# A convolution kernel's first image load, issued as 32 rows on one DMA queue and 96 rows on another

## The chip, the cores and the metric

The kernel runs on one core of one Trainium2 chip. The metric is the device time of one execution in microseconds (us); less is better. A core has five engines that run their own programs and meet at semaphores: TensorE (PE, matrix products into PSUM), VectorE (DVE), ScalarE (ACT), GpSimd (POOL) and SyncE (SP). Transfers between the main memory and the on-chip memory (SBUF, 128 partitions) are issued as DMAs by an engine's program and carried out by 16 DMA engines. In the profile "SPq" is SP's own sequencer, where DMAs are issued and semaphores waited for, and likewise for the other engines.

## The reference

A 3 x 3 convolution with padding 1 over 16 images of 64 channels and 64 x 64 pixels, to 64 output channels, with a residual added. All in float32:

```python
x_pad = np.pad(x, ((0, 0), (0, 0), (pad, pad), (pad, pad)), mode='constant')
for b, co, ci, kh, kw in ...:
    output[b, co] += weight[co, ci, kh, kw] * x_pad[b, ci, kh:kh+h, kw:kw+w]
return (output + residual).astype(np.float32)
```

The images, the residual and the result have 16.78 MB each.

## The kernel before

**Tiling.** Two images make a pair, which is 128 rows (2 x 64 channels) of 4096 pixels, one row for each SBUF partition, 16 KB a row and 2.1 MB a pair. There are eight pairs. The image pairs are loaded into three buffers `xr[0..2]` in turn (`NXR = 3`); the residual lies in one tile `ro` that holds all eight pairs and receives the result in place, so it is also what is stored. ACT casts each image to bfloat16 in two halves (even and odd pixel rows, L174 and L178) into one of four buffers `xp`. PE multiplies: for each image six weight tiles, each against four chunks of eight packed rows (L221 to L238). DVE adds the result in PSUM to the residual (L203), in two halves for each image.

**The weights.** `wraw` holds the raw weights (128 rows of 1152 bytes). PE transposes them in nine steps with an identity matrix that POOL builds (L216), and ACT and DVE copy the results as bfloat16 into `wl` (L183 and L190). The first product of the convolution needs `wl` and the first two casts.

**SP's program.** SP issues every DMA. For each pair p it issues the image load (`load_x`, L72), and after pairs 0, 1, 3, 5 and 7 a residual load (`load_ro`, L77), which brings one or two pairs. Right behind the load of pair 0 stands the weight load (L138). From pair 3 on SP first waits until the casts of pair p-3 have read its buffer (L135). After the loads it issues the stores (L80): three of two pairs each, each behind a wait for DVE's adds, and two of one pair at the end.

**The front.** Programs begin with a short preamble, in which each engine comes to a barrier with a drain; the kernel's own instructions follow it. The function `to_the_front` takes the DMA issued last, removes it from where it stands and inserts it into the first block of the program, ahead of that engine's own drain (L112 to L119):

```python
front = nc.main_func.blocks[0].instructions
at = next(
    i for i, e in enumerate(front) if e.engine == ins.engine and isinstance(e, mybir.InstDrain)
)
```

Before, only the load of pair 0 is moved so, in SP's program (L137).

**The semaphores of the image loads.** Each buffer `xr[i]` has a semaphore `s_x[i]`, to which each finished load adds 16. ACT waits for it ahead of the even image of a pair (L173), for 16 times the number of loads that the buffer has seen.

Of the kernel before, what the change touches and what calls it, by code (L numbers as in the profile page):

```python
# [15 lines left out]
def kernel(  # L16
# [7 lines left out]
    nc = tc.nc  # L24
# [11 lines left out]
    NXR = 3  # L36
# [7 lines left out]
    x_bc = x.rearrange("b c h w -> (b c) (h w)")  # L44
# [7 lines left out]
    xr = [nc.alloc_sbuf_tensor(f"xr{i}", [128, NPIX], FP32) for i in range(NXR)]  # L52
# [8 lines left out]
    s_x = [sem(f"s_x{i}") for i in range(NXR)]  # L61
# [6 lines left out]
    s_conv = sem("s_conv")  # L68
    s_add = sem("s_add")

    def load_x(p):
        return nc.sync.dma_start(out=xr[p % NXR][:, :], in_=x_bc[128 * p : 128 * p + 128, :]).then_inc(s_x[p % NXR], 16)  # L72

    def load_ro(i):
        if i >= 2:
            nc.sync.wait_ge(s_r[i % 2], 16 * (i // 2))
        nc.sync.dma_start(out=ro[:, RES[i], :], in_=res_bc[:, RES[i], :]).then_inc(s_r[i % 2], 16)  # L77

    def store(pairs):
        return nc.sync.dma_start(out=out_bc[:, pairs, :], in_=ro[:, pairs, :])  # L80

    def matmul(out_, lhsT, rhs, start, stop, ldweights):

        e = nc.tensor
        if ldweights:
            return e.matmul(out=out_, lhsT=lhsT, rhs=rhs, start=start, stop=stop, skip_group_check=True)  # L86
        return e.add_instruction(  # L87
            mybir.InstMatmult(
                name=nc.get_next_instruction_name(),
                engine=PE,  # L90
                ins=[e.lower_ap(rhs), e.lower_ap(lhsT)],
                outs=[e.lower_ap(out_)],
                start_tensor_calc=start,
                stop_tensor_calc=stop,
                tile_size=(128, 128),
                tile_position=(0, 0),
                bass_skip_group_check=True,
                ldweights=False,
            )
        )  # L100

    def to_the_front(dma):

        def fixed(ap):
            t = ap.bass_ap.tensor.name
            return mybir.PhysicalAccessPattern(
                ap=ap.ap, offset=ap.bass_ap.offset, dtype=ap.dtype, memref=t, memsetref=t + "_set", bass_ap=ap.bass_ap
            )  # L110

        front = nc.main_func.blocks[0].instructions  # L112
        here = nc.cur_bb.bb.instructions
        ins = here.pop()
        assert ins.name == dma.ins.name
        at = next(
            i for i, e in enumerate(front) if e.engine == ins.engine and isinstance(e, mybir.InstDrain)
        )
        front.insert(at, copy.replace(ins, ins=[fixed(a) for a in ins.ins], outs=[fixed(a) for a in ins.outs]))  # L119
# [5 lines left out]
    def weight_block(h, half, d, par, kh):  # L125

        at = 64 * half + 32 * h
        return dict(out=wl[at : at + 32, d, :, par, :], in_=tp[0:32, kh, 0:384].rearrange("p (kw co h) -> p kw co h", kw=3, h=2)[:, :, :, h])

    with tc.tile_critical(no_gpsimd_drain=True):  # L130

        for p in range(NPAIR):
            if p >= NXR:

                nc.sync.wait_ge(s_half, 2 * (p - NXR) + 3)  # L135
            if p == 0:
                to_the_front(load_x(p))  # L137
                nc.sync.dma_start(out=wraw[:, :], in_=w_rows[:, :]).then_inc(s_w, 16)  # L138
            else:
                load_x(p)  # L140
            if p in (0, 1, 3, 5, 7):
                load_ro((p + 1) // 2)
        for k in range(NEARLY):
            nc.sync.wait_ge(s_add, 4 * k + 5)
            store(slice(2 * k, 2 * k + 2)).then_inc(s_out, 16)


        nc.gpsimd.memset(ident[:, :], 0.0).then_inc(s_id, 1)  # L148
        nc.gpsimd.wait_ge(s_id, 1)
        nc.gpsimd.affine_select(  # L150
            out=ident[:, :],
            in_=ident[:, :],
            compare_op=mybir.AluOpType.not_equal,
            fill=1.0,
            base=0,
            pattern=[[-1, 128]],
            channel_multiplier=1,
        ).then_inc(s_id, 1)
        nc.gpsimd.wait_ge(s_id, 2)
        for t in xp:  # L160
            nc.gpsimd.memset(t[0:64, 0, :], 0.0).then_inc(s_id, 1)  # L161
            nc.gpsimd.memset(t[64:128, J, :], 0.0).then_inc(s_id, 1)  # L162
        nc.gpsimd.memset(wl[0:64, 0, :, 1, :], 0.0).then_inc(s_id, 1)  # L163
        nc.gpsimd.memset(wl[64:128, 1, :, 0, :], 0.0).then_inc(s_id, 1)  # L164


        for n in range(B):
            p, im = divmod(n, 2)
            hp = slice(64 * im, 64 * im + 64)
            x4 = xr[p % NXR].rearrange("q (j two w) -> q j two w", two=2, w=W)  # L170
            t = xp[n % NXP]
            if im == 0:
                nc.scalar.wait_ge(s_x[p % NXR], 16 * (p // NXR + 1))  # L173
            i = nc.scalar.copy(out=t[64:128, 0:J, :], in_=x4[hp, :, 0, :])  # L174
            i.then_inc(s_half, 1)
            if n >= NXP:
                i._wait_ge(s_conv, n - NXP + 1)
            nc.scalar.copy(out=t[0:64, 1 : J + 1, :], in_=x4[hp, :, 1, :]).then_inc(s_pack, 1)  # L178
            if n == 0:
                nc.scalar.wait_ge(s_id, NZERO + 1)  # L180
                for b in blocks[4:]:
                    for h in range(2):
                        i = nc.scalar.copy(**weight_block(h, *b))  # L183
                i.then_inc(s_id, 1)


        nc.vector.wait_ge(s_id, NZERO + 1)
        for k, b in enumerate(blocks[:4]):
            for h in range(2):
                i = nc.vector.tensor_copy(**weight_block(h, *b))  # L190
                if k == h == 0:
                    i.then_inc(s_bank, 2)
        i.then_inc(s_id, 1)
        for n in range(B):
            p, im = divmod(n, 2)
            hp = slice(64 * im, 64 * im + 64)
            o4 = ro[:, p, :].rearrange("q (j two w) -> q j two w", two=2, w=W)
            psj = ps[n % 2].rearrange("q c j w -> q (c j) w")
            if im == 0:
                i = next(i for i, pairs in enumerate(RES) if p < pairs.stop)  # L200
                nc.vector.wait_ge(s_r[i % 2], 16 * (i // 2 + 1))
            for par in range(2):
                i = nc.vector.tensor_tensor(  # L203
                    out=o4[hp, :, par, :], in0=psj[64 * par : 64 * par + 64, :, :], in1=o4[hp, :, par, :], op=ADD
                )
                if par == 0:
                    i._wait_ge(s_conv, n + 1)

                i.then_inc(s_add if par == 0 or n == B - 1 else s_bank, 1)


        nc.tensor.wait_ge(s_id, NZERO)
        nc.tensor.wait_ge(s_w, 16)
        wraw3 = wraw.rearrange("p (ci t) -> p ci t", t=9)
        for t in range(9):
            i = nc.tensor.transpose(  # L216
                out=tp[0:32, t // 3, 128 * (t % 3) : 128 * (t % 3) + 128], in_=wraw3[:, :, t], identity=ident[:, :]
            )
        i.then_inc(s_id, 1)
        nc.tensor.wait_ge(s_id, NZERO + 3)  # L220
        with nc.Fori(0, B // NXP, 1, engines=[PE]):  # L221
            for n in range(NXP):
                nc.tensor.wait_ge(s_bank, 1).then_inc(s_bank, -1)
                nc.tensor.wait_ge(s_pack, 1).then_inc(s_pack, -1)  # L224
                order = [(1, 0), (1, 1), (0, 0), (0, 1), (2, 0), (2, 1)]
                for i, (kw, d) in enumerate(order):
                    xlo, xhi = max(0, 1 - kw), min(W, W + 1 - kw)
                    for c in range(NCHUNK):
                        j0 = JC * c
                        m = matmul(  # L230
                            ps[n % 2][:, c, :, xlo:xhi],
                            wl[:, d, kw, :, :].rearrange("q r c -> q (r c)"),
                            xp[n][:, j0 + d : j0 + d + JC, xlo + kw - 1 : xhi + kw - 1],
                            i == 0,
                            i == len(order) - 1,
                            c == 0,
                        )
                m.then_inc(s_conv, 1)  # L238
# [37 lines left out]
```

## Time and profile before

| | |
|---|---|
| median of 3 runs | 122.76 us (122.69 to 122.91) |
| the profiled execution | 122.68 us |
| its span, first to last instruction | 120.8 us |
| PE busy (matmuls) | 87.9 us, 73% |
| DVE busy | 76.0 us, 63% |
| ACT busy | 63.1 us, 52% |
| POOL busy | 2.4 us, 2% |
| bytes moved by DMA | 50.48 MB: 33.70 read, 16.78 written |
| DMA packets | 3504, of which 304 are under 512 bytes |
| DMAs issued | 19, all by SP, on one queue |

The span is what the trace covers; about 1.9 us of the time lie outside it. The page divides the span into 40 slices of 3.02 us and gives for each the share in which each engine was busy, in tenths, and what the DMA engines moved. A query can give the same for windows of any length; there a DMA packet is counted where it begins, so a short window can show more than the engines can carry. For a DMA the trace has the time that its issue took on the engine's sequencer, and the time from the issue to the landing of its last byte. The first casts of the images run on ACT from 7.79 us, the transposes of the weights on PE from 8.27, and the first product of the convolution from 13.78; the last add ends at about 104.3 us.

### The profile page before, as it was taken

The numbers are of one execution on the slowest core, as the hardware profiler recorded it, in microseconds if no ns is written. First come the engines' busy times: TensorE is split into PE (matmuls) and PEld (weight loads), VectorE is DVE, ScalarE is ACT, GpSimd is POOL, SyncE is SP. The second block draws the span as 40 slices with busy tenths as digits, with TensorE's granted clock in tenths as the row PEclk, the third lists the DMA queues.
The fourth block names the chain that finished last, engine by engine and source line by source line (L and its number), as shares of the span: only waits on it lengthen the run. The fifth ranks groups of instructions, "written<-read, shape, count | busy, mean of one in ns | idle before, by whom it ended". The sixth has DMA issues, their size and how long they took to land.

```text
span 120.8 us, 734 instructions
## 1 busy us (share of the span) xinstructions
PE 87.9 (73%) x393; PEld 10.7 (9%) x105; DVE 76.0 (63%) x40; ACT 63.1 (52%) x37; POOL 2.4 (2%) x16
## 2 busy tenths in 40 slices
PE   0024499999999999999999999999999990000000
PEld 0011001101010011011111111011111100000000
DVE  0005400789898988989879898988989879500000
ACT  4049959948999923999960999883000000000000
POOL 5200000000000000000000000000000000000000
PEclk9999999999999999999999999999999999855555
DMA  7999999999999999999999999999999999999994
GB/s 168 428 428 428 428 428 434 428 434 434 428 434 434 434 428 434 434 434 434 434 434 423 423 428 434 423 412 434 434 434 434 423 434 434 434 428 434 434 434 174
DMA packets 3504, 50.48 MB, mean 418 GB/s; under 512 B 304, under 2 KB 432, under 8 KB 432
## 3 DMA queue, kind: packets, MB, share of 16 engines
q1 hardware_dynamic: 3504, 50.48, 98.5%
HBM read 33.70 MB, written 16.78 MB: 418 GB/s over the span
## 4 chain that ended last, share of the span: by engine, by line
PE 71%; DVEq 2%; DVE 2%; issue 0%
PE ps L87 53%; PE ps L86 18%; DVEq L130 2%; DVE ro L203 2%
## 5 line engine op out<-in xcount | busy, mean ns | idle before, releaser
L203 DVE TENSOR_TENSOR ro<-ps,ro 64x2048 f32<-64x2048 f32 x32 | 73.2, 2289 | 17.7 <-PE ps L87 17.2
L87 PE MATMUL ps<-xp,wl 128*128 128x504 bf16 (+1 forms) x288 | 80.0, 388 | 0.0
L86 PE MATMUL ps<-xp,wl 128*128 128x504 bf16 (+1 forms) x96 | 37.4, 389 | 3.4 <-PEq L224 3.4
L174 ACT CAST xp<-xr 64x2048 bf16<-64x2048 f32 x16 | 30.3, 1896 | 18.3 <-DMA xr<-in_x_dram 17.2
L178 ACT CAST xp<-xr 64x2048 bf16<-64x2048 f32 x16 | 30.4, 1897 | 0.4
L86 PEld LDWEIGHTS ps<-xp,wl 128*128 128x128 bf16 x96 | 9.5, 99 | 79.1 <-issue 79.1
L190 DVE CAST wl<-ps 32x192 bf16<-32x192 f32 x8 | 2.8, 348 | 10.6 <-PE ps L216 10.5
L216 PE MATMUL ps<-ident,wraw 128*32 128x128 f32 x9 | 2.1, 413 | 8.3 <-DMA wraw<-in_weight_dram 8.3
L216 PEld LDWEIGHTS ps<-ident,wraw 128*32 128x32 f32 x9 | 1.2, 137 | 8.7 <-issue 8.2
L174 ACT ACT_TABLE_LOAD x1 | 1.3, 1283 | 1.0 <-SPq L130 1.0
L183 ACT CAST wl<-ps 32x192 bf16<-32x192 f32 x4 | 1.2, 306 | 0.0
L162 POOL MEMSET xp<- 64x64 bf16 x4 | 0.6, 147 | 0.2
L161 POOL MEMSET xp<- 64x64 bf16 x4 | 0.6, 145 | 0.2
L150 POOL TENSOR_SCALAR_AFFINE_SELECT ident<-ident 128x128 f32<-128x128 f32 x1 | 0.3, 294 | 0.2 <-POOL ident L148 0.2
L164 POOL MEMSET wl<- 64x192 bf16 x1 | 0.3, 253 | 0.1
L163 POOL MEMSET wl<- 64x192 bf16 x1 | 0.3, 252 | 0.1
L148 POOL MEMSET ident<- 128x128 f32 x1 | 0.2, 205 | 0.6 <-SPq L130 0.6
L260 POOL MEMSET const-bfloat16-1.0<- 128x1 bf16 x1 | 0.1, 112 | 0.0
L260 POOL MEMSET const-uint8-127<- 128x1 uint8 x1 | 0.1, 112 | 0.0
L260 POOL MEMSET const-float32-0.0<- 128x1 f32 x1 | 0.1, 105 | 0.2 <-issue 0.2
L260 POOL MEMSET const-float32-1.0<- 128x1 f32 x1 | 0.1, 109 | 0.0
## 6 DMA issues: line engine op xcount, KB each, us to landing
xr<-in_x_dram SPq DMA_DIRECT2D x8, 2048.0 KB, 15.3
ro<-in_residual_dram SPq DMA_DIRECT2D x3, 4096.0 KB, 24.0
out_dram<-ro SPq DMA_DIRECT2D x3, 4096.0 KB, 33.2
ro<-in_residual_dram SPq DMA_DIRECT2D x2, 2048.0 KB, 15.9
out_dram<-ro SPq DMA_DIRECT2D x2, 2048.0 KB, 12.8
wraw<-in_weight_dram SPq DMA_DIRECT2D x1, 144.0 KB, 7.1
```

The lines of the kernel that those rows point to most:

```text
L86: return e.matmul(out=out_, lhsT=lhsT, rhs=rhs, start=start, stop=stop, skip_group_check=True)
L87: return e.add_instruction(mybir.InstMatmult(name=nc.get_next_instruction_name(), engine=PE, ins=[e.lower_ap(rhs), e.lower_ap(lhsT)], outs ...
L130: with tc.tile_critical(no_gpsimd_drain=True):
L161: nc.gpsimd.memset(t[0:64, 0, :], 0.0).then_inc(s_id, 1)
L162: nc.gpsimd.memset(t[64:128, J, :], 0.0).then_inc(s_id, 1)
L174: i = nc.scalar.copy(out=t[64:128, 0:J, :], in_=x4[hp, :, 0, :])
L178: nc.scalar.copy(out=t[0:64, 1 : J + 1, :], in_=x4[hp, :, 1, :]).then_inc(s_pack, 1)
L183: i = nc.scalar.copy(**weight_block(h, *b))
L190: i = nc.vector.tensor_copy(**weight_block(h, *b))
L203: i = nc.vector.tensor_tensor(out=o4[hp, :, par, :], in0=psj[64 * par : 64 * par + 64, :, :], in1=o4[hp, :, par, :], op=ADD)
L216: i = nc.tensor.transpose(out=tp[0:32, t // 3, 128 * (t % 3) : 128 * (t % 3) + 128], in_=wraw3[:, :, t], identity=ident[:, :])
L260: nc = _bacc.Bacc("TRN2", target_bir_lowering=False, num_devices=1)
```

## The change

The load of pair 0 becomes two DMAs. Rows 0 to 31 (0.52 MB) are issued by SP, in the place where the whole load was issued; rows 32 to 127 (1.57 MB) are issued by ACT, on ACT's own queue, and are moved in the same way to the front of ACT's program, ahead of its drain in the preamble. Both add 16 to `s_x[0]` when they are done. So the counts for which ACT waits rise by 16 for the pairs that use buffer 0 (pairs 0, 3 and 6). The loads of the other pairs, the weight load, the residual loads and the stores are as before, and so is all that the engines compute.

```diff
-    def load_x(p):
-        return nc.sync.dma_start(out=xr[p % NXR][:, :], in_=x_bc[128 * p : 128 * p + 128, :]).then_inc(s_x[p % NXR], 16)
+    def load_x(p, engine=nc.sync, rows=slice(0, 128)):
+        return engine.dma_start(
+            out=xr[p % NXR][rows, :], in_=x_bc[128 * p + rows.start : 128 * p + rows.stop, :]
+        ).then_inc(s_x[p % NXR], 16)
...
             if p == 0:
-                to_the_front(load_x(p))
+                to_the_front(load_x(p, rows=slice(0, 32)))
                 nc.sync.dma_start(out=wraw[:, :], in_=w_rows[:, :]).then_inc(s_w, 16)
...
+        to_the_front(load_x(0, nc.scalar, slice(32, 128)))
         for n in range(B):
...
             if im == 0:
-                nc.scalar.wait_ge(s_x[p % NXR], 16 * (p // NXR + 1))
+                nc.scalar.wait_ge(s_x[p % NXR], 16 * (p // NXR + 1 + (p % NXR == 0)))
```

## The prediction

> **What bounds the kernel now.** I read the page's slices first, then its queue table and chain, then the start of the span in narrow windows, then the timelines of SP and ACT there, and last the end of the span.
>
> ```profile
> DMA  7999999999999999999999999999999999999994
> GB/s 168 428 428 428 428 428 434 428 434 434 428 434 434 434 428 434 434 434 434 434 434 423 423 428 434 423 412 434 434 434 434 423 434 434 434 428 434 434 434 174
> ...
> q1 hardware_dynamic: 3504, 50.48, 98.5%
> ...
> PE 71%; DVEq 2%; DVE 2%; issue 0%
> ```
>
> The slices say that the 16 DMA engines carry 412 to 434 GB/s in every slice but the first and the last, and the queue table that the one queue's packets fill 98.5% of them. The whole traffic, 50.48 MB, at the best slice's 434 GB/s is 116.3 us of a span of 120.8. The chain of waits names the matmuls (71%), but it ends early, in the last add and the drain behind it, and says nothing of the last 15 us: PE and DVE are at 0 there while the DMA row is still at 9. The bound is therefore the bytes; what is left to win or lose is the time in which the DMA engines do not run at full rate, and that lies at the two ends. The start in windows of 1 us (columns: window, its length, the busy time of the five engines, TensorE's clock, DMA share, GB/s):
>
> ```profile
> 0.00:1.00 1.00, 0.00 (x0) 0.00 (x0) 0.00 (x0) 0.04 (x1) 0.22 (x5) 1.00 0.00 0
> 1.00:2.00 1.00, 0.00 (x0) 0.00 (x0) 0.00 (x0) 1.00 (x1) 0.66 (x4) 1.00 1.62 295
> 2.00:3.00 1.00, 0.00 (x0) 0.00 (x0) 0.00 (x0) 0.24 (x1) 0.73 (x6) 1.00 0.58 213
> 3.00:4.00 1.00, 0.00 (x0) 0.00 (x0) 0.00 (x0) 0.00 (x0) 0.78 (x4) 1.00 0.90 377
> 4.00:5.00 1.00, 0.00 (x0) 0.00 (x0) 0.00 (x0) 0.00 (x0) 0.00 (x0) 1.00 1.07 459
> ...
> 119.00:120.00 1.00, 0.00 (x0) 0.00 (x0) 0.00 (x0) 0.00 (x0) 0.00 (x0) 0.50 0.05 16
> ```
>
> Nothing moves for the first 1.0 us, and then there is a slow start: by 4.0 us 295 + 213 + 377 = 885 KB have been begun where 3 us at 434 GB/s are 1302 KB. That is 417 KB short, about 1.0 us of DMA time, lost once and never regained, since the engines are full from there on. After 119 us nearly nothing moves. So the profiled time, 122.68 us, is: 1.88 outside the span, 1.0 before the first byte, 1.0 of slow start, 116.3 of bytes, about 0.7 of small dips along the way (119.0 - 118.3), and 1.8 from 119.0 to the span's end. The median of the runs, 122.76, is 0.08 above the profiled run.
>
> The issues that set the order at the start, from the timeline of the first 22 us (start, duration, engine, line, what; in brackets the idle time before it and what ended it):
>
> ```profile
> 0.00 0.38 SPq L72 DMA_DIRECT2D xr<-in_x_dram  x1
> ...
> 0.96 1.28 ACT L174 ACT_TABLE_LOAD   x1 [0.96 <-SPq L130]
> 1.00 0.33 SPq L138 DMA_DIRECT2D wraw<-in_weight_dram  x1
> ...
> 1.38 0.57 SPq L77 DMA_DIRECT2D ro<-in_residual_dram  x1
> ...
> 7.79 1.90 ACT L174 CAST xp<-xr 64x2048 bf16<-64x2048 f32 x1 [5.55 <-DMA xr<-in_x_dram]
> ```
>
> The first load costs SP 0.38 us at the span's first instant, and 0.62 us later its first bytes move. All the rest of SP's program, and ACT's table load, comes after a barrier at about 0.96 us.
>
> [...]
>
> **The change part by part.** *SP's issue.* It stays one instruction; at 0.33 to 0.57 us an issue, whatever the bytes (144 KB took 0.33), I expect no saving from fewer rows. From below, the issue could shrink to a quarter, 0.1 us, a gain of at most 0.28 us on the first byte; from above, nothing. I take nothing, and the first byte at 1.0 us as before.
>
> *ACT's issue.* One added DMA instruction of about 0.38 us ahead of ACT's part of the barrier. ACT shows nothing else there, so the barrier moves by 0 to 0.4 us. Behind it wait SP's weight load, the residual load and the second image load, ACT's table load (1.28 us, needed at 7.79, over 5 us spare) and POOL's memsets (done by 3.9, the transposes wait until 8.27). [...] The weight load, issued at up to 1.4 us [...] is in time. Cost nothing[...].
>
> *The semaphore.* Two DMAs now add 32 for pair 0, so the counts of pairs 0, 3 and 6 rise by 16. The wait stands on ACT where it stood; nothing is added behind it.
>
> *The order of arrival.* [...] The image so comes about when it did (7.8) or up to 1.5 us later with the losses below; the weights, which are no longer behind all eight image packets, about with it. The compute has cover for this: SP reissues for pair 3 only at 19.81, when the load of pair 2, issued by 3.5 us, is still landing (its issue to landing is 24.6 us, so at about 27.6); that is some 7 us of queued bytes, 6 after the 1 us from issue to bytes. At the other end the last two stores are issued at 104.6 and 105.0, and the first of them takes 10.5 us to land for 2 MB, which are 4.8 us of bytes: over 4 us of older bytes were queued. A compute chain 1.5 us later empties no queue and costs nothing.
>
> *The ports.* This is where the bytes themselves can be slower. [...] But in the slow start, windows of 0.1 us show that all 16 engines begin one packet between 1.0 and 1.3 us and only some 15 more begin between 1.3 and 3.0[...] so most of this is hidden and I put it at nothing. [...] Six rounds are 1.2 us at the most; the two beside SP's rows I count as hidden by the slow start, four leave 0.8; [...] I take a quarter off: **+0.6 us**. Both ends: 0 [...] and 1.2 + 1.2 = 2.4 us if nothing is hidden. An engine that is late there stays late to the end, because the queues never run empty.
>
> *Slow start.* It may have nothing to do with the queue (0), or be relieved by two rings (at most the whole 1.0 us gained). I take 0.
>
> Sum: 122.68 + 0 (issues) + 0 (semaphore, compute) + 0.6 (ports) = 123.28; 0.08 for the median gives 123.36, and I say 123.3 us.
>
> **The rivals.** *Port crowding*, the forecast: 123.3, own range 122.95 to 124.2. For it: a full-rate DMA with no idle time after 4 us has no slack in which to hide crowding. Against it: nothing in the trace shows a partial-partition load.
>
> *Neutral*: the same 50.48 MB over the same engines, 8 image packets for each[...]: 122.75, within 122.5 to 123.0. For it: the 98.5% and the first byte at 1.0 us, neither of which the change need touch.
>
> *Faster, the slow start is relieved*: its place is the stretch from 1.0 to 4.0 us. [...] Half of the loss regained is 0.5 us, with up to 0.1 to 0.2 for a shorter issue: 122.76 - 0.6 = 122.15, range 121.6 to 122.45. It decides from the point at which the bytes begun by 4.0 us rise by more than about 110 KB (0.25 us x 434 GB/s). Against it: the loss looks the same for all engines and ends at about 3 us[...].
>
> *A second queue costs something outside the span*: at the launch or in the barrier before the first byte[...]: about 123.8. Nothing in before speaks for or against; the 1.88 us outside the span hold only one queue's share.
>
> **How the numbers follow.** Chances: crowding 0.50, neutral 0.22, faster 0.22, the cost of the queue 0.06. Under 0.2% (0.25 us) a measurement of this kernel tells little from nothing. Faster 0.22; same 0.22; slower 0.50 + 0.06 = 0.56. The range leaves out half of the faster case (0.11) and the top of the crowding and the queue case (0.08): 122.1 to 124.2.
>
> **What would show it.** A second queue in the queue table with 1.57 MB. In the first windows: bytes still begin at 1.0; for crowding, the windows from 4 to 9 us stay below 434 GB/s and the last bytes fall after 119.3; for the faster case the windows from 1 to 4 us rise over 885 KB and the last bytes fall before 118.8; for neutral both sums stay. The first cast on ACT may start anywhere from 7.8 to 9.3 without meaning for the time. The image and weight landings, and a weight load issued at 1.0 to 1.4, test the barrier. I am wrong in kind if the first byte comes much earlier, or if the span is the same and the time is not.

## The result, and the profile after

The changed kernel takes 126.27 us (median of 5 runs, 126.23 to 126.41) against 122.86 for the kernel before (5 runs, 122.69 to 122.91): slower by a factor of 1.0284, with a 95% interval of 1.027 to 1.0298, or 3.4 us. The forecast said slower, but by 0.6 us, and 126.27 lies above its range of 122.1 to 124.2. The profiled execution has a span of 124.4 us instead of 120.8.

The page of the changed kernel, its slices and its queue table:

```profile
DMA  7998999999999999999999999999999999999993
GB/s 179 242 262 291 421 427 421 453 453 437 421 421 421 421 427 427 448 453 437 421 421 421 427 421 437 448 442 437 421 421 421 427 427 442 453 437 421 427 421 169
...
q1 hardware_dynamic: 3408, 48.91, 93.0%
q10 hardware_dynamic: 112, 1.57, 5.5%
```

The second queue is there with its 1.57 MB. The three slices after the first, from 3 to 12 us, carry 242, 262 and 291 GB/s where before they carried 428; from the fifth on all is as it was. Yet the DMA row reads 9, 9 and 8 there: the engines are not idle, their packets are slow. The queue table says how slow: 5.5% of 16 engines over 124.4 us is 109 us of engine time for 96 packets of 16 KB, 1.14 us each, where a packet at full rate takes 0.61.

How much of the 3.4 us this is, two windows show, the first 12.2 us and nearly all of the rest (columns: window, length, TensorE's clock, DMA share, GB/s). Before:

```profile
0.00:12.20 12.20, 1.00 0.94 363
12.20:118.00 105.80, 0.94 1.01 431
```

After:

```profile
0.00:12.20 12.20, 1.00 0.95 244
12.20:118.00 105.80, 0.95 1.01 431
```

The second windows are equal. In the first, (363 - 244) GB/s x 12.2 us = 1.45 MB fewer were begun, and 1.45 MB at 431 GB/s are 3.4 us: the whole difference. In windows of 1 us the changed kernel's start reads:

```profile
1.00:2.00 1.00, 1.00 1.04 295
2.00:3.00 1.00, 1.00 1.19 262
3.00:4.00 1.00, 1.00 0.96 229
4.00:5.00 1.00, 1.00 1.15 262
5.00:6.00 1.00, 1.00 1.15 262
6.00:7.00 1.00, 1.00 1.21 263
...
9.00:10.00 1.00, 1.00 0.72 158
10.00:11.00 1.00, 1.00 1.36 376
```

The first byte comes at 1.0 us as before, and up to 3 us the two kernels are alike (557 KB begun by then, 508 before). But where before rose to 459 GB/s at 4 us, the changed kernel carries 158 to 263 GB/s in every window from 2 to 10 us. And its timeline:

```profile
0.00 0.39 SPq L72 DMA_DIRECT2D xr<-in_x_dram  x1
0.12 0.37 ACTq L72 DMA_DIRECT2D xr<-in_x_dram  x1
...
1.08 1.28 ACT L177 ACT_TABLE_LOAD   x1 [1.08 <-SPq L132]
1.12 0.35 SPq L140 DMA_DIRECT2D wraw<-in_weight_dram  x1
...
11.44 1.90 ACT L177 CAST xp<-xr 64x2048 bf16<-64x2048 f32 x1 [9.07 <-DMA xr<-in_x_dram]
11.71 2.08 PE L219 MATMUL ps<-ident,wraw 128*32 128x128 f32 x9 [11.71 <-DMA wraw<-in_weight_dram]
```

ACT's added issue moves the barrier by 0.12 us, as the table load and the weight load show; that is all it costs. The first cast and the transposes start 3.6 and 3.4 us later than before. That delay is not what lengthens the run: no slice from the fifth to the last but one falls below 421 GB/s, so the queues never ran empty while the compute was late.

### The profile page after: what moved, and what is told of

Same layout as the page of the kernel before. It is cut to its first block, busy times and chain, and to the rows that moved or that the text cites. A ratio compares the mean times of both kernels' runs of the same rounds, so it can differ in the third digit from the quotient of the medians.

```text
span 124.4 us, 735 instructions
## 1 busy us (share of the span) xinstructions
PE 87.5 (70%) x393; PEld 10.7 (9%) x105; DVE 76.0 (61%) x40; ACT 63.1 (51%) x37; POOL 2.4 (2%) x16
## 3 DMA queue, kind: packets, MB, share of 16 engines
q10 hardware_dynamic: 112, 1.57, 5.5%
## 4 chain that ended last, share of the span: by engine, by line
PE 69%; DVEq 2%; DVE 2%; issue 0%
PE ps L89 51%; PE ps L88 17%; DVEq L132 2%; DVE ro L206 2%
```

## The experiments

The theories: **place**, the prediction's own ("ports" there and in the expectations), in which the packets of a load into part of the partitions are slow because of which partitions they write; **queue**, in which ACT's queue, or a second queue beside SP's, is slow; **memory**, in which the rows are read badly; and **start**, in which the loss belongs to the program's first transfers. The times of single packets, here and below, are those of the packet records of each run's trace, where one packet of an image load is one row (16 KB, unless the load is split by columns). Where a run is compared with "before", it is with runs of the kernel before that were taken together with it. Each kernel below differs from the changed one in the load of pair 0 alone unless it says otherwise; where the number of DMAs changes, so does the count for which ACT waits.

**The whole load on ACT's queue.**

```diff
-                to_the_front(load_x(p, rows=slice(0, 32)))
...
-        to_the_front(load_x(0, nc.scalar, slice(32, 128)))
+        to_the_front(load_x(0, nc.scalar))
```

> The whole load of pair 0, 128 rows in one DMA, issued by ACT at its front, nothing of it by SP: two queues are in use, but no load of fewer than 128 partitions. Ports theory (a load into fewer than 128 partitions [...] each 16 KB packet takes 1.13 us instead of 0.61): the first image lands at about 8 us and the time is that of before, 122.6 to 123.2 us. Queue theory (ACT's queue[...] runs at half rate): ACT's eight packets for each engine at 1.13 us make the first image land after 10.5 us, and the time is 126 us or more.

122.96 us, 1.0013 times before (1.0003 to 1.0023). Its windows:

```profile
3.00:4.00 1.00, 1.00 0.98 410
4.00:5.00 1.00, 1.00 1.04 442
5.00:6.00 1.00, 1.00 0.97 414
```

Full rate from 3 us on, on ACT's queue. What it costs, 0.16 us, is about the 0.12 us by which ACT issues later than SP (its first packet begins at 1.13 us instead of 1.01). Neither ACT's queue nor a second queue beside SP's is to blame: q10's 2.10 MB take 4.9% of the engines' time here, where its 1.57 MB took 5.5% in the changed kernel.

**Both parts on SP's queue.**

```diff
                 to_the_front(load_x(p, rows=slice(0, 32)))
+                to_the_front(load_x(p, rows=slice(32, 128)))
...
-        to_the_front(load_x(0, nc.scalar, slice(32, 128)))
```

> The same two loads of 32 and 96 rows, both issued by SP at its front, none by ACT: one queue. Ports theory: the packets of the first image take 1.13 us as in the changed kernel, it lands at about 10.5 to 11.5 us, and the time is 126.0 to 126.6 us. Queue theory: with one queue the rate is full, the image lands at about 8 us and the time is 122.6 to 123.3 us.

126.16 us (1.0277, 1.0253 to 1.0301). With one queue the loss is all there:

```profile
5.00:6.00 1.00, 1.00 1.09 262
6.00:7.00 1.00, 1.00 1.19 262
7.00:8.00 1.00, 1.00 1.10 262
8.00:9.00 1.00, 1.00 1.19 262
```

The two runs together put the loss on the split by rows into blocks of partitions and take it from the queues.

**Two queues, split by columns.**

```diff
-            out=xr[p % NXR][rows, :], in_=x_bc[128 * p + rows.start : 128 * p + rows.stop, :]
+            out=xr[p % NXR][:, cols], in_=x_bc[128 * p : 128 * p + 128, cols]
...
-                to_the_front(load_x(p, rows=slice(0, 32)))
+                to_the_front(load_x(p, cols=slice(0, 1024)))
...
-        to_the_front(load_x(0, nc.scalar, slice(32, 128)))
+        to_the_front(load_x(0, nc.scalar, slice(1024, NPIX)))
```

> Pair 0 split by columns: all 128 rows, 1024 of 4096 columns (4 KB a row) on SP's queue and 3072 (12 KB a row) on ACT's, both at the front. Bytes on each queue as in the changed kernel, but each DMA has 128 partitions. Ports theory: full rate, 122.5 to 123.2 us; whether two rings shorten the slow start is open, by 0.5 us at the most. Queue theory: 125.5 us or more.

123.01 us (1.0022, 1.0011 to 1.0032). Its second queue:

```profile
q10 hardware_dynamic: 144, 1.57, 3.1%
```

The same 1.57 MB as in the changed kernel take 3.1% of the engines' time instead of 5.5%. The question left open there is answered too: two queues ("rings" there) do not relieve the slow start. Its windows up to 4 us show 197, 229 and 479 GB/s, 905 KB, against 885 before, and the time is no shorter. In what order the two queues were served shows here too: up to 2.6 us 72 rows of SP's queue begin and 1 of ACT's, but between 3 and 5 us 48 of SP's and 53 of ACT's, about one for one.

**Halves, one on each queue.** Rows 0 to 63 on SP's queue, 64 to 127 on ACT's (the two slices changed, nothing else).

> Pair 0 split by rows into halves: 0 to 63 on SP's queue[...] and 64 to 127 on ACT's[...]. Ports theory: [...] the time is as in the changed kernel, 126.0 to 126.6 us; [...] the time lies between, 123.5 to 125.5 us. Queue theory, by bytes on ACT's queue (1.05 MB instead of 1.57): a loss of two thirds, about 125 us.

127.05 us (1.0349, 1.0329 to 1.037), 0.45 above the range for queues that are served one after the other. The packet records show SP's 64 packets first, at about 1.28 us from the third sixteen on, and then ACT's 64 at 1.17 to 1.25: the two queues were not served in turn here. Split so over two queues, both halves were slow.

**Four blocks of 32 rows, on SP's queue alone.**

```diff
+    def load_part(p, r):
+        return nc.sync.dma_start(
+            out=xr[p % NXR][32 * r : 32 * r + 32, :], in_=x_bc[128 * p + 32 * r : 128 * p + 32 * r + 32, :]
+        ).then_inc(s_x[p % NXR], 16)
...
-                to_the_front(load_x(p, rows=slice(0, 32)))
+                for r in range(4):
+                    to_the_front(load_part(p, r))
...
-        to_the_front(load_x(0, nc.scalar, slice(32, 128)))
```

> Pair 0 in four DMAs of 32 rows, all on SP's queue: partitions 0-31, 32-63, 64-95, 96-127 in turn. Ports theory: [...] packets take 1.13 us, the time is as in the changed kernel, 126.0 to 126.8 us. Size theory (it is the 96 rows [...]): near before, 122.7 to 123.5 us.

**The same number of rows in each, but every fourth one.**

```diff
-            out=xr[p % NXR][32 * r : 32 * r + 32, :], in_=x_bc[128 * p + 32 * r : 128 * p + 32 * r + 32, :]
+            out=xr[p % NXR][r : 128 : 4, :], in_=x_bc[128 * p + r : 128 * p + 128 : 4, :]
```

> Pair 0 again in four DMAs of 32 rows on SP's queue, but each takes every fourth partition, 0, 4, ..., 124 and so on[...]. Ports theory: full rate, 0.61 us a packet after the slow start, 122.6 to 123.3 us. A theory in which any DMA of 32 rows runs at half rate, whatever its partitions: 126.0 to 126.8 us as with four blocks. Memory theory [...]: rows 64 KB apart could be faster or slower, not told apart here.

**Every fourth partition written, neighbouring rows read.**

```diff
-            out=xr[p % NXR][r : 128 : 4, :], in_=x_bc[128 * p + r : 128 * p + 128 : 4, :]
+            out=xr[p % NXR][r : 128 : 4, :], in_=x_bc[128 * p + 32 * r : 128 * p + 32 * r + 32, :]
```

> As the four DMAs with every fourth partition, but each reads 32 neighbouring rows from memory, as the four blocks do; the rows of pair 0 so stand in a different order in the buffer, and the convolution of the first two images mixes their channels. All work is done. Against the four blocks only the partitions written differ. Ports theory: 122.6 to 123.3 us. Memory theory: the reads are those of the four blocks, 126.0 to 126.8 us.

Blocks: 126.87 us (1.0334, 1.0286 to 1.0382), just above the range of the place theory. Every fourth: 124.16 (1.0114, 1.0084 to 1.0143). Every fourth written, neighbours read: 123.73 (1.0077, 1.0037 to 1.0118). The blocks in windows of 2 us:

```profile
2.00:4.00 2.00, 1.00 1.18 246
4.00:6.00 2.00, 1.00 0.94 197
6.00:8.00 2.00, 1.00 0.92 197
8.00:10.00 2.00, 1.00 1.29 262
```

The last of the three, which reads the very same rows in the same order:

```profile
2.00:4.00 2.00, 1.00 0.94 385
4.00:6.00 2.00, 1.00 1.02 270
6.00:8.00 2.00, 1.00 0.91 348
8.00:10.00 2.00, 1.00 1.10 464
```

Only the partitions written differ between these two, and 3.1 us go: nearly all of the loss depends on which partitions are written, which rules the memory theory out for it. Both strided kernels came out above the 122.6 to 123.3 us that the place theory gave, by 0.9 and 0.4 us. Part of this is the first packet, which begins at 1.32 and 1.34 us instead of the blocks' 1.01; their four issues also take SP 2.45 us instead of 1.78. The dip to 270 GB/s from 4 to 6 us, where the third DMA begins, was not explained.

**Pair 1 split instead, on SP's queue, pair 0 whole.**

```diff
-                to_the_front(load_x(p, rows=slice(0, 32)))
+                to_the_front(load_x(p))
...
+            elif p == 1:
+                load_x(p, rows=slice(0, 32))
+                load_x(p, rows=slice(32, 128))
             else:
                 load_x(p)
```

> Pair 0 as before in one load; the load of pair 1, in the middle of a full queue, is split by rows into 32 and 96, both on SP's queue. Ports theory: eight packets for each engine at 1.13 instead of 0.61 us, a loss of 8 x 0.52 = 4.2 us with no slow start to cover a part of it: 126.5 to 127.3 us. A theory in which the loss belongs to the start of the program (first transfers, the preamble, the barrier): no loss, 122.6 to 123.2 us.

127.5 us (1.0385, 1.0349 to 1.0421), 4.8 more than before and 0.2 above the range of the place theory. The loss moves with the load:

```profile
10.00:12.00 2.00, 1.00 0.95 410
12.00:14.00 2.00, 1.00 1.04 262
14.00:16.00 2.00, 1.00 1.12 262
16.00:18.00 2.00, 1.00 1.13 254
18.00:20.00 2.00, 1.00 0.96 221
20.00:22.00 2.00, 1.00 0.80 180
22.00:24.00 2.00, 1.00 0.96 410
```

So it is not the program's start. In the middle of a full queue it costs more; that a slow start no longer covers the first packets is the reason that the expectation gave, and fits: 4.2 us by its estimate, 4.8 measured.

**Which rows are slow, and why the loss has this size.** Five runs had this for their question. Their expectations set two estimates of the packets' time against each other; what these rest on no run shows. All have the DMAs on SP's queue at the front; the edit is the list of slices, for the first

```diff
-                to_the_front(load_x(p, rows=slice(0, 32)))
+                for rows in (slice(32, 96), slice(0, 32), slice(96, 128)):
+                    to_the_front(load_x(p, rows=rows))
```

> Pair 0 in three DMAs on SP's queue: first rows 32 to 95 (64 rows[...]), then 0 to 31 and 96 to 127. [...] the first DMA [...] runs at full rate, so only the two blocks of 32 rows lose[...] and the time is 124.3 to 125.2 us. [...] the time is as with four blocks, 126.4 to 127.2 us.

for the second 0 to 111 and 112 to 127,

> Pair 0 in two DMAs on SP's queue, 112 rows [...] and 16 rows ([...] partitions 112 to 127[...]). [...] For the 112: [...] packets spread from 0.61 to 1.2 us with a mean of about 0.8, and the time is 124.5 to 126.0 us. [...] all packets near 1.13 us, 126.8 to 127.8 us.

for the third 0 to 79 and 80 to 127,

> Pair 0 in two DMAs on SP's queue, 80 rows ([...] partitions 0 to 79) and 48 rows ([...] partitions 80 to 127[...]). The 48 rows run at half rate in any case, 3 x 0.52 = 1.6 us lost. For the 80: [...] packets spread from 0.61 to 1.2 us with a mean of about 0.85 and the time is 124.5 to 125.8 us; [...] all packets are near 1.13 us and the time is 126.0 to 126.9 us.

for the fourth 36 to 99, then 0 to 35 and 100 to 127,

> Pair 0 in three DMAs on SP's queue, rows 36 to 99 first, then the rest (0 to 35 and 100 to 127). Only the first one's packets are looked at[...]. [...] 14 of 16 packets in a round near 0.61 us and two near 1.2. [...] all packets near 1.2 us. The time is not compared, since the rest is dealt in 36 and 28 rows.

and for the fifth 48 to 111, then 0 to 47 and 112 to 127.

> The same with rows 48 to 111 first[...]. [...] half of the packets in a round near 0.61 us and half near 1.2. [...] all near 1.2 us. [...]

The times: 125.19 (rows 32 to 95 first; 1.0182, 1.0164 to 1.02), 126.89, 128.6, 128.6 and 130.45 us. The first lies at the top of the lower range, the one in which the 64 rows run at full rate. Rows 0 to 111 have a time that only the upper range allowed, but packets that it did not (0.61 to 1.14 us, not all near 1.13); and rows 0 to 79 took 1.7 us more than either, because the 48 rows behind them ran at 1.72 to 2.12 us a packet instead of the 1.13 assumed. The first run, in windows:

```profile
3.00:4.00 1.00, 1.00 0.98 410
4.00:5.00 1.00, 1.00 1.04 377
5.00:6.00 1.00, 1.00 1.26 262
6.00:7.00 1.00, 1.00 1.17 262
7.00:8.00 1.00, 1.00 1.25 262
```

Up to nearly 5 us the 64 rows run at 377 to 410 GB/s, then the two blocks of 32 at 262. The table takes from the packet records of each trace the time of packets in the steady part of a partial load:

```
rows of the DMA         us of one packet
32 to 95   (64 rows)    0.61 to 0.64, all
36 to 99   (64 rows)    0.61 to 0.66, few of 0.72 to 1.38
0 to 111   (112 rows)   0.61 to 1.14, mean of the sixteens 0.73 to 1.07
32 to 127  (96 rows)    1.04 to 1.24, all
48 to 111  (64 rows)    1.17 to 1.25, all
0 to 79    (80 rows)    1.11 to 1.20, all
0 to 63    (64 rows)    1.27 to 1.29, all
80 to 127  (48 rows)    1.72 to 2.12, all
112 to 127 (16 rows)    1.11 to 1.78 behind rows 0 to 111,
                        1.86 to 2.13 behind rows 0 to 47
```

Two things can be read from it. The number of rows does not decide: 64 rows stand at 0.61 to 0.64 us, at 1.17 to 1.25 and at 1.27 to 1.29. And in six of the loads all packets are slow: of the 96 rows none took under 1.04 us, of the 48 none under 1.72. Two loads are mixed, rows 36 to 99 with few slow packets and rows 0 to 111 in between. So neither estimate of the last two expectations holds for both: of rows 36 to 99 most packets were fast, of rows 48 to 111 none was.

What makes a block of partitions slow, and how rows are shared out among the DMA engines, no run here shows: a packet record tells a packet's queue, start, time and size. The loads that reach over all 128 partitions, with every fourth or every second row or whole, ran mostly at 0.61 to 0.65 us a packet after the start.

**Two queues, every other row.** The version that keeps the split by rows but lets each part reach from the first partitions to the last:

```diff
-                to_the_front(load_x(p, rows=slice(0, 32)))
+                to_the_front(load_x(p, rows=slice(0, 128, 2)))
...
-        to_the_front(load_x(0, nc.scalar, slice(32, 128)))
+        to_the_front(load_x(0, nc.scalar, slice(1, 128, 2)))
```

> Pair 0 split by rows over both queues, as in the changed kernel, but every other row: 0, 2, ..., 126 on SP's queue and 1, 3, ..., 127 on ACT's, 64 rows each, both at the front. [...] Ports theory: the loss of the changed kernel is gone, 122.7 to 123.6 us[...]. A theory in which any split by rows over the two queues costs: 126.0 us or more.

123.31 us, 1.0034 times before (1.002 to 1.0047). The loss is nearly gone with two queues and half of the rows on each. The queue table's line for ACT's queue, in the halves and then here, with the same number of rows, bytes and packets:

```profile
q10 hardware_dynamic: 80, 1.05, 3.9%
```

```profile
q10 hardware_dynamic: 80, 1.05, 2.0%
```

The first packet begins at 1.36 us instead of 1.01, which is most of the 0.4 us that is left. No version was faster than before.

## Why the prediction was right in kind and wrong in size

- *What bounds the kernel*: right. All of the difference lies in bytes per microsecond up to 12.2 us.
- *SP's issue, ACT's issue, the semaphore*: right. First byte at 1.0 us, barrier 0.12 us later, nothing behind it late for it.
- *The order of arrival*: the image came 3.6 us later, not up to 1.5, but the cover held, as argued. "About with it" was right of the weights, but the two queues were not served in turn from the start, on which the author had counted. The weight load was issued at 1.12 us, but its first packet began at 6.7, when 58 of ACT's 96 rows had begun. Up to 10 us 29 weight packets then began beside ACT's other 38 rows, and the remaining 99 after 10. The traces show one queue's packets begin alone at first (ACT's 58 here) and those of both after that (29 weight packets beside 38 rows here, 48 rows beside 53 with the split by columns); what sets the change is open.
- *The ports*: that a load into part of the partitions can be slow is borne out, and its size is the term that failed: it was put at **0.6 us** and measures 3.4. The 0.6 was the author's estimate, and what it rested on was not shown. Its parts, by the mean packet times of the first sixteen packets, the second and so on: SP's two rounds were put at nothing because the slow start hides them, and that held: 0.92 + 1.16 us against 1.44 + 0.80 before. ACT's six rounds were put at 1.2 us at the most, 0.20 above full rate for each; measured are 1.11, 1.14, 1.15, 1.20, 1.07 and 1.17, together 6.84 us against 3.69 in the same six rounds before, so 0.53 a round. All packets of the 96 rows took 1.04 to 1.24 us, so none ran at full rate. Of the six rounds the prediction counted four, two being "beside SP's rows"; but they came after SP's rows, and all six cost. And the quarter taken off was wrong, since of SP's packets only 29 weight packets of 1152 bytes, and no residual packets, came in between. Six rounds at 0.53 are 3.2 us; 0.15 less for SP's rounds, 0.15 more for the first residual packets (0.76 instead of 0.61) and some 0.3 more for the eight weight packets (about 0.09 us each instead of 0.05) make 3.5, against 3.4 measured.
- *The upper end* of 2.4 us came from the same estimate and so was no bound.
- *The rivals*: the slow start is the same with one queue or two (885 KB begun by 4 us before, 905 with columns), the queue costs nothing outside the span (1.8 us lie outside with the whole load on ACT's queue, 1.9 before), and neutral falls with the result.
- The sign that the prediction named, windows from 4 to 9 us below 434 GB/s and last bytes after 119.3, is what the profile shows (from 122 to 123 us still 246 GB/s).

## What to carry to other kernels

Split a transfer that sets the pace by columns, or by rows with a step, and not by blocks of partitions: 32 and 96 rows of one 2 MB load cost 3.4 us where columns cost at most 0.4, every second row 0.4, and four loads of every fourth row 1.0 to 1.4. A block of partitions is not always slow: rows 32 to 95 took 0.61 to 0.64 us a packet, as the whole load does. The time of a partial load can't be had from the number of its rows: a packet took 0.61 to 2.13 us in the blocks measured, and no rule for other blocks was shown. A second queue gained nothing here, where the one queue's packets already filled 98.5% of the engines' time.

## What the runs showed of the hardware that was not expected

- Partial loads depend on where they lie: 64 rows ran at 0.61 to 0.64 us a packet from partition 32, at about 1.23 from 48 and 1.28 from 0.
- Two queues were not served row by row in turn from the start: after SP's 32 rows came the first 58 of ACT's 96, and SP's next packets, ready since about 2.1 us (an estimate, from the 1.0 us from issue to first byte at the start), began at 6.7 us at the earliest and mostly after 10. With the whole load on ACT's queue it was the same: 82 of ACT's 128 rows had begun before the first weight packet, at 5.14 us.
- Where the first DMA had 64 rows (five kernels) or a step of four partitions (two), its first packet began at 1.32 to 1.41 us; where it had 128, 112, 80 or 32 neighbouring rows and SP issued it, at 1.00 to 1.03. Part of it is the issue: with 64 rows on SP's queue beside 64 on ACT's it took SP 0.55 or 0.56 us instead of 0.38 or 0.39, and the barrier behind it came 0.57 us later than in the changed kernel. The rest is open.
- A DMA with a step of four partitions took SP 0.61 us to issue (2.45 for four), blocks of the same 32 rows 0.45 (1.78 for four).
